# Last chunk of a Strassen MLP on Trainium2: a new order of the products, accumulating DMAs for the additions, the residual added in the output

## The chip, the cores and the metric

One core of one Trainium2 chip runs the kernel. The metric is the device time of one execution in microseconds (us), lower is better. TensorE (PE) multiplies, VectorE (DVE), ScalarE (ACT) and GpSimd (POOL) do the elementwise work, and DMAs are issued from the queues of SyncE (SP), ACT and POOL. Only a DMA issued on POOL adds to its destination here (`accum_op`).

## What is computed

One layer of an encoder over x of 512 x 2048 float32: convolution and attention, then the part that the change touches, the MLP:

```python
x = x + rms_norm(mix, post_mix_g[l])
h = rms_norm(x, pre_mlp_g[l])
f = jnp.square(jax.nn.relu(h @ w_up[l])) @ w_down[l]
x = x + rms_norm(f, post_mlp_g[l])
```

The last `rms_norm` needs the sum of squares over a whole row of 2048 columns of `f`; the row is then scaled by `r` (the reciprocal root) and by `post_mlp_g`, and the x of the line before (the residual, "x1" in the code) is added.

## The kernel before

**Chunks.** The MLP runs over 8 chunks of 1024 hidden columns. A chunk first makes its hidden block (`up`, two groups `g`), then multiplies it with its rows of `w_down` by a Strassen scheme of seven products, the table `PROD` (L30). The output f is cut into four quadrants (t, n): t = 0 holds rows 0 to 255 (row blocks of 128, j = 0 and 1), t = 1 the lower rows (j = 2 and 3), n the halves of 1024 columns. An entry of `PROD` names a ring buffer or the four Q tiles as weight source ("r" or "q"), the quarters of `w_down` that are summed, the form of the hidden block (a21, a11, t2, t5, t1, a22, t4), and the quadrants to which the product is added, with signs:

```python
PROD = (("q", (0, 0), "a21", {(1, 0): 1, (1, 1): -1}),
        ("r", ((0, 1), (1, 1)), "a11", {(0, 0): -1, (0, 1): 1}),
        ("q", (0, 1), "t2", {(1, 1): 1}),
        ("r", ((1, 1),), "t5", {(0, 1): -1, (1, 1): 1}),
        ("q", (1, 1), "t1", {(0, 0): 1, (1, 1): -1}),
        ("r", ((1, 0),), "a22", {(0, 0): -1, (1, 0): 1}),
        ("q", (1, 0), "t4", {(0, 0): 1}))
```

**One product** is four `down` steps of 12 matmuls; a step uses one weight piece of 128x1024 (half `nb` of the columns, half `h` of the depth). All numbers are float32 as a high and a low part: `ensure` (L196) makes them for a piece, a copy on ACT (L133) and a subtraction on DVE (L212). A ring holds three such pieces, so the split of piece s+2 stands ahead of step s. When a piece is split, `send_next` issues the next load into its buffer: a plain load on SP (L178), an accumulating one on POOL (L176). `split_form` (L746) splits the form, `sums` (L751) makes the next form in place.

**Adding products up.** After two steps half a product lies in two PSUM banks. `evac_down` (L784) takes it: in chunk 0 ACT copies it to one of seven accumulators, in chunks 1 to 6 DVE adds it, and in chunk 7 DVE adds or subtracts it to each quadrant `CA[q]` that `PROD` names (L794). Before chunk 7's products, `fold` combines the seven accumulators into the four quadrants; X[1] and X[2] are then free.

**The end.** Products run in the order 0 to 6 in chunk 7 also. Product 6 is left as four `fin` steps, one per row block j of the upper rows and half of the columns; its four pieces (blocks of Q) are split into Ah and Al. For a unit of 128x512, `stat` (L806) squares and sums on ACT, `gain` (L809) multiplies by `post_mlp_g` on POOL (on DVE for the last), and `finish_row` (L814) makes `r` by `tot_rstd` and writes x1 + r * m, three units of a row on DVE (L822) and one on ACT and POOL (L820), and stores them (L812). x1 of all four row blocks was stored to DRAM (`x1d`) ahead of the MLP and is read back by `load_x1` (L827) at the start of chunk 7's products.

**Order.** Each engine runs its instructions in the order in which the Python loop over `steps` emits them; `bg` adds work after a given step. A DMA in a queue waits for its semaphores with all that stands behind it.

Of the kernel before, what the change touches and what calls it, by code (L numbers as in the profile page):

```python
# [16 lines left out]
P = 128  # L17
# [48 lines left out]
def encoder_layer(ctx, tc, xT, xp, wst, pk, gmix, gmlp, rawb, maskc, out):  # L66
# [65 lines left out]
    def copy(o, i, scale=1.0):  # L132
        act(o, i, AF.Copy, scale=scale)  # L133
# [100 lines left out]
    for c in range(NCH):  # L234
        for g in range(2):
            fp = add_pieces(16, 2, 512, gain=True, mod=12)
            k0 = 0
            if c == 0 and g == 0:
                steps.append(dict(kind="up0", c=c, g=g, k=3, p=fp, n=16, cost=10.4))
                k0 = 4  # L240
            for k in range(k0, 16):
                steps.append(dict(kind="up", c=c, g=g, k=k, p=fp + k, n=16, cost=2.6))
        base = nw[0]
        nw[0] += 16
        quarter = lambda r, n, nb, h: base + 8 * r + 4 * n + 2 * nb + h
        for i, (buf, quarters, form, signs) in enumerate(PROD):
            last = c == NCH - 1 and i == NP - 1
            fp = len(pieces)
            for nb in range(2):
                for h in range(2):  # L250
                    if buf == "q":
                        b = add_block(("q", nb, h), [(quarter(*quarters, nb, h), i > 0)])
                    else:
                        b = add_block(None, [(quarter(*x, nb, h), n_ > 0) for n_, x in enumerate(quarters)])
                    res = None
                    if last:
                        e = 4 * nb + 2 * h
                        res = (Ah[:, e:e + 2, :].rearrange("p a b -> p (a b)"), Al[:, e:e + 2, :].rearrange("p a b -> p (a b)"))
                    add_piece(b, 0, 1024, None, res, 12)
            if last:  # L260
                for u in range(4):
                    steps.append(dict(kind="fin", c=c, i=i, tb=u // 2, nb=u % 2, p=fp, n=4, k=u, cost=2.6))
            else:
                for u in range(4):
                    steps.append(dict(kind="down", c=c, i=i, nb=u // 2, h=u % 2, p=fp + u, n=4, k=u, cost=2.6))
    n_ring = 0
    for blk in blocks:
        if not isinstance(blk["slot"], tuple):
# [490 lines left out]
    PREP = {(0, 1): lambda: sums("t5"), (0, 2): lambda: sums("d"), (0, 3): lambda: sums("t2"),  # L759
            (1, 1): lambda: split_form(2), (2, 1): lambda: split_form(3), (2, 2): lambda: sums("t1"),  # L760
            (3, 1): lambda: split_form(4), (3, 2): lambda: sums("t4"), (4, 1): lambda: split_form(5),
            (5, 1): lambda: split_form(6)}

    def up_set(c, g):
        return 4 * ((c + g) % 2)
# [15 lines left out]
    def hv(a, nb):  # L781
        return a[:, 1024 * nb:1024 * nb + 1024]

    def evac_down(c, i, nb):  # L784
# [18 lines left out]
    x1r = [f(Ah[:, 8 + 4 * j:12 + 4 * j, :]) for j in range(2)] + [f(Al[:, 8 + 4 * j:12 + 4 * j, :]) for j in range(2)]  # L803

    def stat(j, cb):
        act(X[2][:, 0:512], cunit(j, cb), AF.Square, accum_out=ss[:, 4 * j + cb:4 * j + cb + 1])  # L806

    def gain(j, cb, eng=None):
        (eng or nc.gpsimd).tensor_tensor(cunit(j, cb), cunit(j, cb), GM[:, 512 * cb:512 * cb + 512], ALU.mult)  # L809

    def store(j, cb, eng=None):
        (eng or nc.sync).dma_start(out[P * j:P * j + P, 512 * cb:512 * cb + 512], cunit(j, cb))  # L812

    def finish_row(j, last=False):  # L814
        r = tot_rstd(j, 20 if j % 2 else 32)
        for cb in (2, 0, 1, 3) if last else range(4):
            m = cunit(j, cb)
            if cb == 2:
                copy(m, m, r)
                nc.gpsimd.tensor_tensor(m, m, x1r[j][:, cb, :], ALU.add)  # L820
            else:
                V.scalar_tensor_tensor(m, m, r, x1r[j][:, cb, :], ALU.mult, ALU.add)  # L822
            if cb != 2:
                store(j, cb)
        store(j, 2, nc.scalar if last else nc.sync)

    def load_x1():  # L827
        for j in range(4):
            nc.scalar.dma_start(x1r[j], x1d[P * j:P * j + P].rearrange("p (a b) -> p a b", a=4))
        nc.gpsimd.dma_start(GM, bass.AP(tensor=gmlp.tensor, offset=gmlp.offset, ap=[[0, P], [1, D]]))  # L830

    su = first("up0")
    for j in range(4):
        bg.setdefault(su + 2 + j, []).append(lambda j=j: (x1_stat(j), nc.gpsimd.dma_start(x1d[P * j:P * j + P], X[j])))
    bg.setdefault(su + 7, []).append(lambda: rstd(sm[:, 0:4], 4, 1.0 / D, RMS_EPS, 16))
    bg_pe.setdefault(su + 9, []).append(r2_b)
    bg.setdefault(su + 10, []).append(lambda: [send_next(("q", nb, h), -1) for nb in range(2) for h in range(2)])
    for c in range(NCH):
        u1 = first("up", c=c, g=1)
        for i in range(2):  # L840
            bg.setdefault(u1 + 4 + 3 * i, []).append(lambda i=i: split_form(i))
        d0 = first("down", c=c, i=0)
        for (i, k), fn in PREP.items():
            bg.setdefault(d0 + 4 * i + k, []).append(fn)
# [6 lines left out]
    for i, rows, cbs in ((4, (0, 1), (2, 3)), (5, (2, 3), (2, 3)), (6, (2, 3), (0, 1))):  # L851
        for u in range(4):
            j, cb = rows[u % 2], cbs[u // 2]
            bg.setdefault(d7 + 4 * i + u, []).append(lambda j=j, cb=cb: (stat(j, cb), gain(j, cb)))
    for j in (2, 3):
        bg[d7 + 4 * 6 + 3].append(lambda j=j: finish_row(j))
# [4 lines left out]
    for si, s in enumerate(steps):  # L861
# [66 lines left out]
        elif kind == "oseq":  # L928
            j = s["j"]
            tk = slice(P * j, P * j + P)  # L930
            for kk in range(8):
                qq = pieces[p + kk]
                ah, al = Ah[:, 8 + kk, tk], Al[:, 8 + kk, tk]
                mm(acc[j], ah, qq["h"], start=False, stop=False, skip_group_check=True)
                mm(acc[j], al, qq["h"], start=False, stop=False, skip_group_check=True)
                mm(acc[j], ah, qq["l"], start=False, stop=(kk == 7), skip_group_check=True)
            if j >= 1:
                z_transpose(j - 1)
            oseq_post(j)
        elif kind in ("down", "fin"):  # L940
            pr = down_pair(s["c"], s["i"], s["nb"])
            fh, fl = mlp["FH"][s["i"] % 2], mlp["FL"][s["i"] % 2]
            todo = [(s["h"], q, tb) for tb in range(2)] if kind == "down" else [(h, pieces[p + 2 * s["nb"] + h], s["tb"]) for h in range(2)]
            for kk in range(2):
                for h, qq, tb in todo:
                    a = 2 * h + kk
                    fs = slice(P * tb, P * tb + P)
                    wh, wl = qq["h"][:, 512 * kk:512 * kk + 512], qq["l"][:, 512 * kk:512 * kk + 512]
                    st = kk == 0 and h == 0
                    en = kk == 1 and h == 1  # L950
                    mm(B[pr + tb], fh[:, a, fs], wh, start=st, stop=False, skip_group_check=True)  # L951
                    mm(B[pr + tb], fh[:, a, fs], wl, start=False, stop=False, skip_group_check=True)  # L952
                    mm(B[pr + tb], fl[:, a, fs], wh, start=False, stop=en, skip_group_check=True)  # L953
# [29 lines left out]
            elif kind == "up":  # L983
                evac_up(s["c"], s["g"])
        if kind == "down" and k % 2 == 1:
            evac_down(s["c"], s["i"], s["nb"])
        elif kind == "fin":
            j = s["tb"]
            m, b = cunit(j, s["nb"]), B[down_pair(s["c"], s["i"], s["nb"]) + j]
            V.tensor_tensor(m, m, b, ALU.add)  # L990
            stat(j, s["nb"])
            gain(j, s["nb"], V if k == 3 else None)
            if k % 2 == 1:
                finish_row(j, last=k == 3)
# [80 lines left out]
```

## Time and profile before

| What | us |
|---|---|
| Time, median of 3 runs (lowest, highest) | 2090.79 (2087.34, 2091.76) |
| The profiled execution: own time | 2092.75 |
| The profiled execution: span | 2091.0 |
| Start of chunk 7's products | 1981.1 |
| End of the last matmul | 2067.1 |

The profile is of one execution; its span begins with its first instruction, and times in a row count from there. Durations below come from it.

### The profile page before, as it was taken

The page shows a single profiled execution, that of the slowest core. Times are in us where ns is not written, and L with a number is a line of the kernel's source. Part 1 is how long each engine was busy: PE and PEld are TensorE (multiplying, and loading weights), DVE is VectorE, ACT ScalarE, POOL GpSimd, SP SyncE. Part 2 cuts the span into 40 slices and gives each one's busy share as a digit, 9 for nine tenths or more (in the row PEclk, how much of TensorE's full clock was granted, in tenths as well). Part 3 has the DMA queues.
Part 4 walks back from the last instruction along what each step waited for, and adds up shares of the span by engine and source line. Part 5 has one row for each costly group of instructions (what it writes and reads, how often), then busy time and mean ns, then how long its engine had stood idle before and what let it go on. Part 6 is the DMA issues. An engine that isn't in the chain of part 4 may idle for free.

```text
span 2091.0 us, 24692 instructions
## 1 busy us (share of the span) xinstructions
PE 2034.6 (97%) x9423; PEld 1684.8 (81%) x9423; DVE 1324.9 (63%) x1656; ACT 892.7 (43%) x1387; POOL 281.4 (13%) x275
## 2 busy tenths in 40 slices
PE   9999999997999999999999999999999999999994
PEld 7888887887788888888888888888888888888873
DVE  6899896976644644534843853763673573476498
ACT  6334444435653554633433433443343343343353
POOL 5110111112101301101101100100100110110124
PEclk9999999998999999999999999999999999999997
DMA  5223232222324256735844854763763773673592
GB/s 208 97 94 107 78 97 80 94 75 69 102 85 171 91 215 157 191 122 128 197 138 123 184 161 122 175 171 102 170 191 101 158 195 111 151 190 124 136 276 81
DMA packets 78584, 288.43 MB, mean 138 GB/s; under 512 B 8880, under 2 KB 9024, under 8 KB 76672
## 3 DMA queue, kind: packets, MB, share of 16 engines
q1 hardware_dynamic: 55440, 197.16, 27.9%
q0 software_dynamic: 21008, 81.16, 20.1%
q10 hardware_dynamic: 2016, 8.53, 1.1%
q8 instruction: 74, 1.21, 0.2%
q14 instruction: 46, 0.38, 0.1%
HBM read 278.42 MB, written 8.39 MB: 137 GB/s over the span
## 4 chain that ended last, share of the span: by engine, by line
PE 68%; DVE 3%; issue 2%; ACT 1%; POOL 0%; DVEq 0%; ACTq 0%; POOLq 0%
PE PS L898 33%; PE PS L951 9%; PE PS L953 9%; PE PS L952 9%; PE PS L927 2%; PE PS L926 2%; PE PS L925 2%; DVE WL L212 1%; DVE M L822 1%; DVE M L794 0%; PE PS L708 0%; PE PS L571 0%; DVE Al L212 0%; POOL M L679 0%; PE PS L557 0%
## 5 line engine op out<-in xcount | busy, mean ns | idle before, releaser
L898 PE MATMUL PS<-Ah,WH 128*128 128x512 f32 x1176 | 462.1, 393 | 3.7 <-ACT WH L133 3.7
L898 PE MATMUL PS<-Ah,WL 128*128 128x512 f32 x1176 | 459.8, 391 | 0.0
L898 PE MATMUL PS<-Al,WH 128*128 128x512 f32 x1176 | 459.6, 391 | 0.0
L133 ACT ACTIVATE WH<-WR 128x512 fp32r<-128x512 f32 (+2 forms) x312 | 207.4, 673 | 361.3 <-PE PS L898 155.3
L212 DVE TENSOR_TENSOR WL<-WR,WH 128x512 fp32r<-128x512 f32 (+2 forms) x312 | 255.4, 828 | 166.4 <-ACT WH L133 164.2
L215 DVE SCALAR_TENSOR_TENSOR WL<-WR,PRM,WH 128x512 fp32r<-128x512 f32 x170 | 128.2, 760 | 226.2 <-ACT WH L133 226.1
L898 PEld LDWEIGHTS PS<-Ah,WH 128*128 128x128 f32 x1176 | 222.5, 189 | 50.4 <-ACT WH L133 4.4
L898 PEld LDWEIGHTS PS<-Ah,WL 128*128 128x128 f32 x1176 | 222.3, 189 | 46.8
L898 PEld LDWEIGHTS PS<-Al,WH 128*128 128x128 f32 x1176 | 222.7, 189 | 45.4
L951 PE MATMUL PS<-WH,FH 128*128 128x512 f32 x588 | 232.7, 396 | 0.0
L953 PE MATMUL PS<-WH,FL 128*128 128x512 f32 x588 | 232.5, 395 | 0.0
L952 PE MATMUL PS<-WL,FH 128*128 128x512 f32 x588 | 232.1, 395 | 0.0
L133 ACT ACTIVATE WH<-WR,PRM 128x512 fp32r<-128x512 f32 x170 | 122.9, 724 | 246.7 <-PE PS L898 227.0
L212 DVE TENSOR_TENSOR WL<-Q,WH 128x1024 fp32r<-128x1024 f32 x83 | 101.3, 1222 | 97.2 <-ACT WH L133 97.2
L133 ACT ACTIVATE WH<-Q 128x1024 fp32r<-128x1024 f32 x83 | 88.2, 1063 | 136.1 <-PE PS L953 82.0
L215 DVE SCALAR_TENSOR_TENSOR WLX<-WR,PRM,WHX 128x512 fp32r<-128x512 f32 x86 | 64.1, 751 | 121.1 <-ACT WHX L133 121.1
L176 POOL DMA_DIRECT2D Q<-in_wst_dram x96 | 86.5, 901 | 376.0 <-DVE WL L212 238.9
L176 POOL DMA_DIRECT2D WR<-in_wst_dram x32 | 28.0, 875 | 808.5 <-DMA WR<-in_wst_dram 776.4
L898 PE MATMUL PS<-Al,WHX 128*128 128x512 f32 x344 | 135.9, 395 | 0.0
L898 PE MATMUL PS<-Ah,WHX 128*128 128x512 f32 x344 | 135.9, 395 | 0.0
L898 PE MATMUL PS<-Ah,WLX 128*128 128x512 f32 x344 | 135.6, 394 | 0.0
L953 PEld LDWEIGHTS PS<-WH,FL 128*128 128x128 f32 x588 | 110.2, 187 | 27.2
(200 smaller groups left out, 3506.7 us busy)
## 6 DMA issues: line engine op xcount, KB each, us to landing
WR<-in_wst_dram SPq DMA_DIRECT2D x335, 512.0 KB, 3.5
Q<-in_wst_dram POOLq DMA_DIRECT2D x96, 512.0 KB, 5.9
Q<-in_wst_dram SPq DMA_DIRECT2D x32, 512.0 KB, 3.6
WR<-in_wst_dram POOLq DMA_DIRECT2D x32, 512.0 KB, 5.7
X<-in_xp_dram POOLq DMA_DIRECT2D x4, 1024.0 KB, 8.9
x1d<-X POOLq DMA_DIRECT2D x4, 1024.0 KB, 9.3
out_dram<-M SPq DMA_DIRECT2D x15, 256.0 KB, 2.4
M<-in_xT_dram ACTq DMA_DIRECT2D x7, 512.0 KB, 4.7
```

Source lines behind the costliest of these rows:

```text
L133: act(o, i, AF.Copy, scale=scale)
L176: nc.gpsimd.dma_start(t, wst[i], accum_op=ALU.add)
L212: V.tensor_tensor(l, raw, f(h), ALU.subtract)
L215: V.scalar_tensor_tensor(l, raw, q["g"], f(h), ALU.mult, ALU.subtract)
L822: V.scalar_tensor_tensor(m, m, r, x1r[j][:, cb, :], ALU.mult, ALU.add)
L898: mm(acc[n], w, (Al if t == 1 else Ah)[:, k, :], start=(k == 0 and t == 0), stop=(lastk and t == 2), skip_group_check=True)
L925: mm(acc[j], ah[:, tk], q["h"], start=st, stop=False, skip_group_check=True)
L926: mm(acc[j], ah[:, tk], q["l"], start=False, stop=False, skip_group_check=True)
L927: mm(acc[j], al[:, tk], q["h"], start=False, stop=en, skip_group_check=True)
L951: mm(B[pr + tb], fh[:, a, fs], wh, start=st, stop=False, skip_group_check=True)
L952: mm(B[pr + tb], fh[:, a, fs], wl, start=False, stop=False, skip_group_check=True)
L953: mm(B[pr + tb], fl[:, a, fs], wh, start=False, stop=en, skip_group_check=True)
```

## The change

In chunk 7 the products run in the order 0, 2, 3, 4, 5, 1, 6 (`LAST`); "position i" below is the place in that order. At positions 0 to 3, ACT copies the two banks, scaled by the sign, into a half of X[1] or X[2], and a DMA on POOL adds that half to the quadrant; at positions 4 and 5 DVE adds as before. Row blocks 0, 2 and 3 of x1 are stored into `out` itself, and `add_row` adds r * m * gain to them by accumulating DMAs; only row block 1 goes through `x1d` and is finished in SBUF by `last_row`. The lower rows are finished at positions 4 and 5. The form a11 is split early into a free part of Ah and Al.

```diff
+LAST = (0, 2, 3, 4, 5, 1, 6)
-    x1d = drp.tile([T, D], F32, name="x1d")
+    x1d = drp.tile([P, D], F32, name="x1d")
...
+            pi = LAST[i] if c == NCH - 1 else i
+            buf, quarters, form, signs = PROD[pi]
...
+    def form_at(c, i):
+        if c == NCH - 1 and LAST[i] == 1:
+            return [t[:, 8:10, :].rearrange("p a (b c) -> p (a b) c", c=256) for t in (Ah, Al)]
+        return mlp["FH"][i % 2], mlp["FL"][i % 2]
...
+            plan = ((0, 0, 5), (0, 1, "t5"), (0, 2, "d"), (0, 2, "t2"), (0, 3, 1), (1, 1, 2), (1, 2, "t1"), (2, 1, 3), (2, 2, "t4"),
+                    (3, 1, 4), (5, 0, 6))
...
-            for q, sg in PROD[i][3].items():
+            for n_, (q, sg) in enumerate(PROD[pi][3].items()):
                 m = hv(CA[q], nb)
-                V.tensor_tensor(m, m, bank, ALU.add if sg > 0 else ALU.subtract)
+                if i < 4:
+                    st = hv(X[1 + n_], nb)
+                    copy(st, bank, float(sg))
+                    nc.gpsimd.dma_start(m, st, accum_op=ALU.add)
+                else:
+                    V.tensor_tensor(m, m, bank, ALU.add if sg > 0 else ALU.subtract)
...
+    def add_row(j, r, n):
+        V.scalar_tensor_tensor(wide(j, n), wide(j, n), r, gw(n), ALU.mult, ALU.mult)
+        nc.gpsimd.dma_start(out[P * j:P * j + P, 1024 * n:1024 * n + 1024].rearrange("p (a b) -> p a b", a=2), wide(j, n), accum_op=ALU.add)
+
+    def gain(cb):
+        V.tensor_tensor(cunit(1, cb), cunit(1, cb), GM[:, 512 * cb:512 * cb + 512], ALU.mult)
+
+    def last_row():
+        r = rows_rstd(1, 1, 20)
+        for cb in (2, 3, 0, 1):
+            m = cunit(1, cb)
+            V.scalar_tensor_tensor(m, m, r, x1r[:, cb, :], ALU.mult, ALU.add)
+            (nc.sync if cb % 2 else nc.scalar).dma_start(out[P:2 * P, 512 * cb:512 * cb + 512], m)
 
     def load_x1():
-        for j in range(4):
-            nc.scalar.dma_start(x1r[j], x1d[P * j:P * j + P].rearrange("p (a b) -> p a b", a=4))
-        nc.gpsimd.dma_start(GM, bass.AP(tensor=gmlp.tensor, offset=gmlp.offset, ap=[[0, P], [1, D]]))
+        nc.scalar.dma_start(x1r, x1d.rearrange("p (a b) -> p a b", a=4))
+        nc.sync.dma_start(GM, bass.AP(tensor=gmlp.tensor, offset=gmlp.offset, ap=[[0, P], [1, D]]))
...
+    for i, k, fn in [(4, 0, lambda: (stat(2, 2), stat(3, 2))), (4, 2, lambda: (stat(2, 3), stat(3, 3))),
+                     (4, 3, lambda: (stat(2, 0), stat(3, 0))),
+                     (5, 0, lambda: (stat(2, 1), stat(3, 1))), (5, 1, lambda: rows_rstd(2, 2, 32)),
+                     (5, 1, lambda: add_row(2, r23[:, 0:1], 1)), (5, 2, lambda: add_row(3, r23[:, 1:2], 1)),
+                     (5, 2, lambda: add_row(2, r23[:, 0:1], 0)), (5, 3, lambda: add_row(3, r23[:, 1:2], 0)),
+                     (5, 3, lambda: (stat(0, 2), stat(1, 2))), (6, 0, lambda: (stat(0, 3), stat(1, 3), gain(2), gain(3)))]:
```

**Place 1: POOL, the end of its queue.** Before, the last four loads of Q (here Q01 to Q11, for product 6) are followed by GpSimd's own multiplications and additions:

```order
L176 DMA Q01_5387<-in_wst_dram 128x1024 [waits DMASW5_49,DVE_49]
L176 DMA Q10_5388<-in_wst_dram 128x1024 [waits DMASW6_49,DVE_49]
L809 TENSOR_TENSOR M_67<-M_67,X0_68 128x512 [waits DMASW3_49,Activation_49]
L176 DMA Q11_5389<-in_wst_dram 128x1024 [waits DMASW7_49,DVE_49]
L809 TENSOR_TENSOR M_67<-M_67,X0_68 128x512 [waits Activation_49] x11
```

Now, from position 2's second half on (M is where the quadrants lie, X1 and X2 are X[1] and X[2], WR0 to WR3 the ring tiles):

```order
L816 DMA M_67<-X2_70 128x1024 [waits DMASW6_49,DMASW0_49,Activation_49]
L178 DMA Q10_5388<-in_wst_dram 128x1024 [waits DVE_49]
L178 DMA Q11_5389<-in_wst_dram 128x1024 [waits DVE_49]
L816 DMA M_67<-X1_69 128x1024 [waits DMASW1_49,Activation_49]
L816 DMA M_67<-X2_70 128x1024 [waits DMASW2_49,Activation_49]
L178 DMA WR0_73<-in_wst_dram 128x1024 [waits DMAHW1_49,DMASW3_49]
L178 DMA WR1_74<-in_wst_dram 128x1024 [waits DMAHW2_49,DMASW4_49]
L816 DMA M_67<-X1_69 128x1024 [waits DMASW5_49,Activation_49]
L816 DMA M_67<-X2_70 128x1024 [waits DMASW6_49,Activation_49]
L178 DMA WR2_75<-in_wst_dram 128x1024 [waits DMAHW3_49,DMASW7_49]
L178 DMA WR3_76<-in_wst_dram 128x1024 [waits DMAHW4_49,DMASW0_49]
L844 DMA out_0_dram<-M_67 128x2x512 [waits DMASW2_49,DMASW6_49,DMASW1_49,DVE_49]
```

GpSimd's arithmetic is gone; 14 additions of 128x1024 (L816) and 6 into `out` (L844) stand in the queue, and the four accumulating loads of product 1 (WR0 to WR3) come last among the loads.

**Place 2: DVE, from the form of product 6 to the last piece.** Before:

```order
L212 TENSOR_TENSOR Al<-Q_5386,Ah 128x1024
L749 TENSOR_TENSOR FL_5392<-G,FH_5390 128x1024
L794 TENSOR_TENSOR M<-M,PS 128x1024 x2
L212 TENSOR_TENSOR Al<-Q_5387,Ah 128x1024
L212 TENSOR_TENSOR Al<-Q_5388,Ah 128x1024
L794 TENSOR_TENSOR M<-M,PS 128x1024 x2
L212 TENSOR_TENSOR Al<-Q_5389,Ah 128x1024
```

Now, behind the split of WR3, the split of Q00 and the six small instructions that begin the reciprocal root of the lower rows:

```order
L318 TENSOR_TENSOR sm<-sm 128x2
L843 SCALAR_TENSOR_TENSOR M<-M,sm,X_68 128x2x512
L818 TENSOR_TENSOR M<-M,PS 128x1024 x2
L214 TENSOR_TENSOR Al<-Q_5387,Ah 128x1024
L843 SCALAR_TENSOR_TENSOR M<-M,sm,X_68 128x2x512 x2
L214 TENSOR_TENSOR Al<-Q_5388,Ah 128x1024
L843 SCALAR_TENSOR_TENSOR M<-M,sm,X_68 128x2x512
L818 TENSOR_TENSOR M<-M,PS 128x1024 x2
L214 TENSOR_TENSOR Al<-Q_5389,Ah 128x1024
```

The lower rows are scaled (L843) between the splits of the last product's pieces.

## Rows read from the trace of the kernel before

**Rows 1.** The page: span, and its part 1.
```profile
span 2091.0 us, 24692 instructions
...
PE 2034.6 (97%) x9423; PEld 1684.8 (81%) x9423; DVE 1324.9 (63%) x1656; ACT 892.7 (43%) x1387; POOL 281.4 (13%) x275
```
**Rows 2.** Busy time by stretch (stretch, its length, then each engine).
```profile
1981.10:2037.10 56.00, 55.98 (x241) 44.74 (x240) 52.43 (x46) 28.79 (x35) 13.79 (x15) 1.00 0.97 270
2037.10:2067.10 30.00, 24.46 (x95) 18.64 (x95) 26.97 (x27) 13.55 (x27) 14.32 (x10) 0.94 0.04 10
2067.10:2091.00 23.90, 0.01 (x1) 0.00 (x0) 16.65 (x34) 4.83 (x12) 10.01 (x7) 0.59 0.47 174
```
**Rows 3.** The chain of work that ended last: first matmul of chunk 7's products (start, length).
```profile
1981.09 0.23 PE PS L951
```
**Rows 4.** Timeline of ACT in chunk 0, first and last of thirteen evacuations (start, length).
```profile
824.93 1.03 ACT L133 ACTIVATE M<-PS 128x1024 f32<-128x1024 f32 x1 [1.63 <-PE PS L953]
...
889.05 1.06 ACT L133 ACTIVATE WH<-Q 128x1024 fp32r<-128x1024 f32 x1 [0.82 <-PE PS L953]
891.81 1.03 ACT L133 ACTIVATE M<-PS 128x1024 f32<-128x1024 f32 x1 [1.70 <-PE PS L953]
```
**Rows 5.** Timeline of PE in chunk 7: its waits, and the last matmul.
```profile
2039.11 0.50 PE L952 MATMUL PS<-WLX,FH 128*128 128x512 f32 x1 [2.02 <-DVE WLX L212]
...
2053.76 0.50 PE L952 MATMUL PS<-Al,FH 128*128 128x512 f32 x1 [2.51 <-DVE Al L212]
...
2059.38 0.50 PE L952 MATMUL PS<-Al,FH 128*128 128x512 f32 x1 [1.02 <-DVE Al L212]
...
2066.72 0.39 PE L953 MATMUL PS<-Ah,FL 128*128 128x512 f32 x1
```
**Rows 6.** Timeline of DVE in chunk 7.
```profile
1987.36 2.35 DVE L794 TENSOR_TENSOR M<-M,PS 128x1024 f32<-128x1024 f32 x2
1989.62 1.22 DVE L212 TENSOR_TENSOR WL<-WR,WH 128x1024 fp32r<-128x1024 f32 x1
...
2034.35 4.71 DVE L212 TENSOR_TENSOR WLX<-WR,WHX 128x1024 fp32r<-128x1024 f32 x1
...
2076.12 0.14 DVE L682 TENSOR_REDUCE sm<-sm 128x1 f32<-128x4 f32 x1
...
2077.69 3.08 DVE L822 SCALAR_TENSOR_TENSOR M<-M,sm,Al 128x512 f32<-128x512 f32 x3
2080.70 0.67 DVE L990 TENSOR_TENSOR M<-M,PS 128x512 f32<-128x512 f32 x1
2082.22 0.69 DVE L809 TENSOR_TENSOR M<-M,X 128x512 f32<-128x512 f32 x1 [0.85 <-ACT X L806]
...
2084.41 3.08 DVE L822 SCALAR_TENSOR_TENSOR M<-M,sm,Ah 128x512 f32<-128x512 f32 x3
```
**Rows 7.** Timeline of POOL in chunk 7: one of its multiplications.
```profile
2033.88 4.08 POOL L809 TENSOR_TENSOR M<-M,X 128x512 f32<-128x512 f32 x3
```
**Rows 8.** DMA queues from 1975 to 2042 (packets, MB, share of 16 engines), and issues.
```profile
q0 software_dynamic: 2016, 7.87, 58.6%
q10 hardware_dynamic: 576, 4.19, 16.3%
q1 hardware_dynamic: 1152, 4.19, 15.8%
...
Q<-in_wst_dram POOLq DMA_DIRECT2D x12, 512.0 KB, 8.2
```
**Rows 9.** DMA queues from 738 to 742: only the stores of x1 from SBUF run.
```profile
q0 software_dynamic: 222, 1.68, 104.0%
```
**Rows 10.** Timeline of POOL: the last loads of Q for product 2.
```profile
1984.96 0.87 POOL L176 DMA_DIRECT2D Q<-in_wst_dram  x1 [6.18 <-DVE WLX L212]
1986.60 0.87 POOL L176 DMA_DIRECT2D Q<-in_wst_dram  x1 [0.77 <-DVE WL L212]
```
**Rows 11.** Busy time by stretch; the last two numbers are DMA share and GB/s.
```profile
1987.00:1993.00 6.00, 6.00 (x27) 4.87 (x26) 6.00 (x6) 2.63 (x3) 1.03 (x2) 1.00 1.03 340
...
2011.00:2017.00 6.00, 6.00 (x28) 4.85 (x27) 5.93 (x6) 2.12 (x2) 0.00 (x0) 1.00 1.07 226
```
**Rows 12.** The page, part 6: issues (KB each, us from issue to landing).
```profile
WR<-in_wst_dram SPq DMA_DIRECT2D x335, 512.0 KB, 3.5
Q<-in_wst_dram POOLq DMA_DIRECT2D x96, 512.0 KB, 5.9
```

More of the change, by code (lines that the diff above doesn't have):

```diff
@@ L245, in encoder_layer @@
         quarter = lambda r, n, nb, h: base + 8 * r + 4 * n + 2 * nb + h
-        for i, (buf, quarters, form, signs) in enumerate(PROD):
+        for i in range(NP):
+            pi = LAST[i] if c == NCH - 1 else i
+            buf, quarters, form, signs = PROD[pi]
             last = c == NCH - 1 and i == NP - 1
@@ L261, in encoder_layer @@
                 for u in range(4):
[L262 removed]
+                    steps.append(dict(kind="fin", c=c, i=i, pi=pi, tb=u // 2, nb=u % 2, p=fp, n=4, k=u, cost=2.6))
             else:
                 for u in range(4):
[L265 removed]
+                    steps.append(dict(kind="down", c=c, i=i, pi=pi, nb=u // 2, h=u % 2, p=fp + u, n=4, k=u, cost=2.6))
     n_ring = 0
@@ L757, in sums, with prep @@
         V.tensor_tensor(o, a, b, op)
[L759 to L762, printed above, removed]
+    def prep(c):
+        if c < NCH - 1:
+            for i in range(2):
+                yield first("up", c=c, g=1) + 4 + 3 * i, lambda i=i: split_form(c, i)
+            plan = ((0, 1, "t5"), (0, 2, "d"), (0, 3, "t2"), (1, 1, 2), (2, 1, 3), (2, 2, "t1"), (3, 1, 4), (3, 2, "t4"),
+                    (4, 1, 5), (5, 1, 6))
+        else:
+            yield first("up", c=c, g=1) + 4, lambda: split_form(c, 0)
+            plan = ((0, 0, 5), (0, 1, "t5"), (0, 2, "d"), (0, 2, "t2"), (0, 3, 1), (1, 1, 2), (1, 2, "t1"), (2, 1, 3), (2, 2, "t4"),
+                    (3, 1, 4), (5, 0, 6))
+        d0 = first("down", c=c, i=0)
+        for i, k, what in plan:
+            yield d0 + 4 * i + k, (lambda what=what: sums(what)) if isinstance(what, str) else (lambda what=what: split_form(c, what))
     def up_set(c, g):
@@ L782, in hv, with evac_down @@
         return a[:, 1024 * nb:1024 * nb + 1024]
[L784 removed]
+    def evac_down(c, i, pi, nb):
         pr = down_pair(c, i, nb)
@@ L802, in encoder_layer @@
     GM = X[0]
-    x1r = [f(Ah[:, 8 + 4 * j:12 + 4 * j, :]) for j in range(2)] + [f(Al[:, 8 + 4 * j:12 + 4 * j, :]) for j in range(2)]
-    def stat(j, cb):
[L806 to L825, printed above, removed]
+    x1r = f(Ah[:, 12:16, :])
@@ new lines, in wide, with gw, rows_rstd @@
+    def wide(j, n):
+        return CA[j // 2, n].rearrange("p (n t c) -> p n t c", n=2, t=2)[:, :, j % 2, :]
+    def gw(n):
+        return GM[:, 1024 * n:1024 * n + 1024].rearrange("p (a b) -> p a b", a=2)
+    def stat(j, cb):
+        act(rb, cunit(j, cb), AF.Square, accum_out=ss[:, 4 * j + cb:4 * j + cb + 1])
+    def rows_rstd(j, n, col):
+        V.tensor_reduce(sm[:, 60:60 + n], ss[:, 4 * j:4 * (j + n)].rearrange("p (a b) -> p a b", b=4), AX.X, ALU.add)
+        return rstd(sm[:, 60:60 + n], n, 1.0 / D, RMS_EPS, col)
@@ L838, in encoder_layer @@
     for c in range(NCH):
[L839 to L844, printed above, removed]
+        for si, fn in prep(c):
+            bg.setdefault(si, []).append(fn)
     u0 = first("up", c=NCH - 1, g=0)
@@ L849, in encoder_layer @@
     bg.setdefault(d7 + 1, []).append(load_x1)
[L851 to L856, printed above, removed]
+    r23 = sm[:, 32:34]
+    for i, k, fn in [(4, 0, lambda: (stat(2, 2), stat(3, 2))), (4, 2, lambda: (stat(2, 3), stat(3, 3))),
[4 more added lines that the diff above has]
+                     (5, 3, lambda: (stat(0, 2), stat(1, 2))), (6, 0, lambda: (stat(0, 3), stat(1, 3), gain(2), gain(3)))]:
+        bg.setdefault(d7 + 4 * i + k, []).append(fn)
     gap_until = 0.0
@@ L991, in encoder_layer @@
             stat(j, s["nb"])
-            gain(j, s["nb"], V if k == 3 else None)
-            if k % 2 == 1:
-                finish_row(j, last=k == 3)
+            if j:
+                gain(s["nb"])
+            if k == 1:
+                r = rows_rstd(0, 1, 20)
+                for n in range(2):
+                    add_row(0, r, n)
+            elif k == 3:
+                last_row()
 def _layout(inputs):
```

18 lines of the change are left out of this document (10 added, 8 removed).

## The prediction

> **What bounds the kernel now.** The page comes first: PE is busy 97% of a span of 2091.0 us [rows 1], so a change in the last chunk can win only where PE waits there, or after its last matmul. The table by stretch shows where that is [rows 2]. Chunk 7's products begin at 1981.1 [rows 3]; I count from there and write T for it, so the span ends at T109.9. Up to 2037.1 PE is busy 55.98 of 56 us; in the next 30 us it lacks 5.5; after 2067.1 it has nothing to do for 23.9. What the seven products cost without a wait is seen in chunk 0, where ACT alone takes the banks: 12 half products lie between two evacuations 66.88 us apart [rows 4], so one is 5.573 and 14 are 78.0. Here the last matmul ends at 2067.1 [rows 5], T86.0: 8.0 us were lost. PE's timeline names for whom: 2.02, 2.51 and 1.02 us, each time for a DVE split [rows 5]; the rest is the slower clock behind a wait (0.94 on the mean) [rows 2]. DVE is busy 52.43 of 56 us and then 26.97 of 30 [rows 2]. Its instruction of 4.71 us, on a shape that takes 1.22 a few rows higher, runs beside GpSimd's multiplications [rows 6, 7]. So DVE is the bound, first by its queue and then by the finish of four row blocks.
>
> **What the change takes away.** At positions 0 to 3 (signs 2, 1, 2, 2, two halves each) 14 additions leave DVE; two cost 2.26 us from start to start [rows 6], 1.13 each, so 15.8 us. ACT takes 14 copies of 1.03 [rows 4]. For a product with two signs it then has four copies, four splits of 1.06 [rows 4] and a form, 9.4 of 11.15 us: it fits if nothing makes it wait. GpSimd's arithmetic goes, and DVE's collisions with it. Three row blocks no longer wait to be finished behind the last matmul.
>
> **The end, if no DMA is late.** The DVE order of place 2 sets it. Position 4 is multiplied at T55.7 (10 half products). DVE then has two additions, the split of WR2, the form of product 6 and the split of WR3: 5 x 1.13, so WR3 is split at T61.4, and PE wants it only at T64.1. Behind it stand four splits, four row scalings (L843; the form is new, priced as an addition of as many elements) and four additions, 12 x 1.13 = 13.6, and a reciprocal root, 1.57 from its first instruction to the scaling behind it [rows 6]: 15.2. Then 1.9 for the eight matmuls that need the last split, and for row block 0 an addition 0.6, its square 0.8, a root 1.5, two scalings 2.3; for row block 1 two rounds of addition, square and gain overlapped to 4.1; a root 1.5, four last operations at 0.67 each 2.7 (three took 3.08 with GpSimd in the way [rows 6]), and 3.5 from DVE's last instruction, 2087.5, to the span's end: 18.9. So **end = split of WR3 + 34.1**, here T95.5, 2076.6: 14.4 us less. PE ends inside the 18.9, at 7.5; it is no longer the bound of the tail. The change breaks even when WR3 is split at T75.8, 14 us late.
>
> **What the DMAs take.** From 1975 to 2042 the software queue moved 7.87 MB in 58.6% of 67 us, 39.3 us of all 16 engines; the plain queue 4.19 MB in 15.8%, 10.6 us [rows 8]. So a plain 512 KB takes 1.32. Of the 7.87 MB, 1.05 are the gains (plain, 2.65 us); the other 6.82 are 13 accumulating loads, 36.6 us: **2.82 each**, twice a plain one. All three queues together took 60.8 of these 67 us: little is free. Shares of 1.03 to 1.07 in saturated stretches [rows 11] say that some 3.5% overlaps.
>
> The price m of an addition from SBUF to SBUF stands in no row. Below it cannot well be under a plain copy: 1.32, or 1.30 by the stores of x1 from SBUF, 1.68 MB at 104% of 4 us [rows 9]. Above, it is the accumulating load of the same shape and queue, 2.82. It reads two things and writes one, as that load does, so it is nearest to it; since SBUF gave its bytes a little faster, I take **m = 2.7**. The Trainium skill says why such a DMA should cost double: the page "Collectives: The Full Stack", section "The bandwidth ceiling", has it that the add is free but needs two source reads on one ring. The accumulating loads here agree (2.82 against 1.32); by that rule m is 2.64 and the end 0.8 us earlier than mine, an estimate. No run here shows it for two sources in SBUF.
>
> **The sum.** The last loads of Q for product 2 are issued at T3.9 and T5.5 [rows 10] and, with x1 of one row block, hold the engines up to T13.8 (2 x 2.82 + 2.65). From there, all in front of or among the loads for product 1, come 8 Q and 4 WR accumulating loads, 33.8; 8 plain WR loads, 10.6; 14 additions, 37.8 (3 MB less of x1 are 7.9 us that the start no longer has). That is 82.2, with the overlap 79.4: WR3 lands at T93.2, where PE wanted it split at T64.1. POOL issues in order, and WR3 is the last load in place 1, so nothing can pass. On the way it shows as ACT waiting: the copy of position 1 into a half of X[1] must wait for the addition of position 0 from it, and behind that copy stands a split. With 2.3 for the split (1.06 and 1.22) WR3 is ready at T95.5, the end is T129.6, **2110.7: 19.7 us more** than 2091.0. The additions into `out` of the lower rows lie beside the last product; those of row block 0 are issued some 11 us before the end and land in 6 to 9 by the loads' 5.9 [rows 12]. The profiled execution's own time is 1.96 above the median of the runs; I move the median 2090.79 by the same 19.7: **2110**.
>
> With m = 1.32 the work is 62.9, with overlap 60.8: WR3 lands at T74.6, is ready at T76.9, end 2092.1, 1.1 more. With m = 2.82 and no overlap: 83.9, WR3 at T97.7, end 2115.2; some us for the slower clock behind long waits and for idle engines while POOL waits lead to 2120.
>
> **Rivals.** First, **faster: the DMAs keep up.** If packets of several accumulating DMAs overlap so that each costs the engines no more than a copy, loads and additions together are 34 x 1.32 = 44.9 and WR3 lands at T58.7, before PE wants it. Then the end is 2076.6, 14.4 us less: 2076. It decides at a landing of T73.5, that is at 60 us for the whole work. For it speaks that ACT kept pace with the copies in chunk 0, and that DVE is plainly the bound now; against it, that the accumulating loads did not overlap so: in the full stretch they landed 8.2 us after issue [rows 8], over the run 5.9 [rows 12]. By the fit in the page "DMA: Bandwidth & Descriptors" of the Trainium skill, section "Anatomy of one DMA", 2 us and then 436 GB/s, 512 KB would move in 1.2 us, which would put this case ahead of mine, an estimate; the trace does not agree for accumulating loads, which land after 5.9 us where plain ones need 3.5 [rows 12]. Second, **no change: only the additions are cheap** (m near 1.32): the gain at the tail is eaten by the late WR3, 2092. Speaks for it that no HBM is read; against it that the destination is read as before. That the change does not do what it says can be left out: both places show the instructions.
>
> **Chances.** Late DMAs as summed: 0.70, own range 2099 to 2120. No change: 0.12, 2088 to 2099. Faster: 0.18, 2072 to 2088. The range that holds 8 in 10 leaves out most of the faster case: 2084 to 2120. A measurement can tell 0.2%, 4.2 us. Faster by more than that takes the faster case and a little of the second: 0.19; within it 0.10; slower the rest, 0.71.
>
> **What would show it.** In the new profile the DMA share should be near 1 from 1990 to 2075, not to 2040; PE should have waits of 5 to 10 us from position 1 on, behind splits on ACT and DVE that themselves wait for DMAs; WR3's split should stand near T95, the last matmul near T118, 15 to 20 us before the end. The forecast is wrong if PE runs through positions 1 to 3 without waits, if an addition takes well under 2 us of the 16 engines, or if the split of WR3 lies before T76.

## The result, and the profile after

The change takes 2114.97 us (median of 4 runs, 2113.48 to 2116.50) against 2090.24 us of the kernel before, run beside it (4 runs, 2087.34 to 2091.76): a ratio of 1.0121, 95% interval 1.0108 to 1.0134. It is slower by 24.7 us where 19.7 was forecast, and inside the range. The profiled execution took 2115.64 us with a span of 2113.8. Its last chunk begins 1.3 us earlier than before's, by the evacuation ahead of the products, here in the change and then before:

```profile
1978.48 2.70 ACT L793 ACTIVATE G<-PS 128x512 f32<-128x512 f32 x4 [3.40 <-DVE PS L792]
```

```profile
1979.76 2.70 ACT L774 ACTIVATE G<-PS 128x512 f32<-128x512 f32 x4 [3.40 <-DVE PS L773]
```

From there to the end it is 135.3 us against 111.2: 24.1 more. Where the last chunk begins differs by some us from one execution to the next, so kernels are compared below by this length, called L, of one execution each (two executions of one kernel, further down, have 99.9 and 100.0).

The page of the change, span and part 1, against [rows 1]:

```profile
span 2113.8 us, 24667 instructions
...
PE 2043.5 (97%) x9423; PEld 1689.3 (80%) x9423; DVE 1299.7 (61%) x1636; ACT 902.5 (43%) x1396; POOL 270.3 (13%) x275
```

DVE's work fell by 25 us, POOL's by 11, and the kernel is slower. Busy time by stretch (PE, PEld, DVE, ACT, POOL, granted clock, DMA share, GB/s), against [rows 2]:

```profile
1981.10:2037.10 56.00, 46.87 (x184) 36.47 (x183) 29.86 (x26) 32.07 (x34) 19.14 (x22) 0.91 0.99 215
2037.10:2067.10 30.00, 18.07 (x65) 13.06 (x63) 6.66 (x6) 6.82 (x10) 4.40 (x5) 0.83 1.06 241
2067.10:2091.00 23.90, 15.65 (x52) 11.73 (x52) 21.05 (x25) 13.21 (x26) 5.71 (x5) 0.85 0.50 78
2091.00:2113.80 22.80, 10.13 (x32) 7.74 (x32) 13.34 (x29) 4.63 (x14) 2.39 (x2) 0.65 0.70 136
```

In the first 86 us no compute engine is full any more: PE 65 of 86 us, DVE 37, where before it had 79. What is full is the last column but one, the DMA engines: 1.06 over 30 us in which they had 0.04 before. The same table in steps of 6 us shows where that begins and ends:

```profile
1987.00:1993.00 6.00, 3.96 (x18) 2.86 (x16) 4.60 (x4) 3.26 (x5) 2.46 (x3) 1.00 1.00 182
...
2059.00:2065.00 6.00, 5.70 (x17) 4.56 (x18) 3.64 (x4) 0.18 (x1) 0.00 (x0) 0.65 1.06 231
2065.00:2071.00 6.00, 2.72 (x10) 1.72 (x9) 1.81 (x2) 4.21 (x10) 0.86 (x1) 0.92 0.76 161
2071.00:2077.00 6.00, 6.00 (x23) 4.81 (x22) 5.71 (x6) 4.76 (x8) 0.00 (x0) 0.80 0.29 58
```

PE's timeline, four of its waits (start, length, in brackets the idle time before it and what ended that), against [rows 5]:

```profile
1993.13 0.50 PE L977 MATMUL PS<-WH,FH 128*128 128x512 f32 x1 [2.17 <-ACT FH L135]
...
2023.99 0.79 PE L977 MATMUL PS<-WH,FH 128*128 128x512 f32 x1 [5.96 <-ACT WH L135]
...
2058.04 0.79 PE L977 MATMUL PS<-WH,FH 128*128 128x512 f32 x1 [10.29 <-ACT WH L135]
...
2083.86 0.80 PE L978 MATMUL PS<-Al,FH 128*128 128x512 f32 x1 [2.77 <-DVE Al L214]
```

The first is for the form of position 1, which waits for sums on DVE and not for a DMA. The two long ones, at positions 3 and 4, wait for splits on ACT. ACT's own timeline says what held those:

```profile
2021.06 1.94 ACT L135 ACTIVATE X<-PS 128x1024 f32<-128x1024 f32 x2 [9.34 <-DMA M<-X]
...
2055.57 0.63 ACT L836 ACTIVATE rb<-M 128x512 f32<-128x512 f32 x1 [11.95 <-DMA M<-X]
...
2066.73 0.63 ACT L836 ACTIVATE rb<-M 128x512 f32<-128x512 f32 x1 [7.55 <-DMA M<-X]
```

`M<-X` is an accumulating addition of the change. At 2021 a copy waits for its staging half; at 2055 and 2066 a square of the statistics waits for a sum that the DMAs have not finished, and the split of the next block stands behind it in ACT's order. Last, product 1's last block on its way, from its accumulating load on POOL to the split on DVE:

```profile
2068.10 0.86 POOL L178 DMA_DIRECT2D WR<-in_wst_dram  x1 [12.64 <-DMA WR<-in_wst_dram]
```

```profile
2075.23 1.23 DVE L214 TENSOR_TENSOR WLX<-WR,WHX 128x1024 fp32r<-128x1024 f32 x1 [0.28 <-ACT WHX L135]
```

The load lands 5.3 us after its issue, at 2073.4. The block is split by 2076.46, T95.4, and the span ends 37.3 us later. The page's part 6 (KB each, median us from issue to landing), against [rows 12]:

```profile
M<-X POOLq DMA_DIRECT2D x14, 512.0 KB, 12.5
```

### The profile page after: what moved, and what is told of

Its sections match the earlier page's. It is cut to its first block, busy times and chain, and to the rows that moved or that the text cites. A ratio compares the mean times of both kernels' runs of the same rounds, so it can differ in the third digit from the quotient of the medians.

```text
span 2113.8 us, 24667 instructions
## 1 busy us (share of the span) xinstructions
PE 2043.5 (97%) x9423; PEld 1689.3 (80%) x9423; DVE 1299.7 (61%) x1636; ACT 902.5 (43%) x1396; POOL 270.3 (13%) x275
## 4 chain that ended last, share of the span: by engine, by line
PE 66%; DVE 3%; DMA 3%; issue 2%; ACT 1%; POOL 0%; DVEq 0%; ACTq 0%; POOLq 0%
PE PS L924 33%; PE PS L977 9%; PE PS L979 9%; PE PS L978 9%; PE PS L953 2%; PE PS L952 2%; PE PS L951 2%; DMA M<-X 1%; DMA WR<-in_wst_dram 1%; DVE WL L214 0%; DVE M L843 0%; DVE M L818 0%; ACT X L135 0%; PE PS L712 0%; PE PS L575 0%
## 5 line engine op out<-in xcount | busy, mean ns | idle before, releaser
L977 PEld LDWEIGHTS PS<-WH,FH 128*128 128x128 f32 x580 | 110.2, 190 | 46.1 <-ACT WH L135 17.5
L978 PEld LDWEIGHTS PS<-WL,FH 128*128 128x128 f32 x580 | 110.0, 190 | 29.4 <-DVE WL L214 3.0
```

## The experiments

All are edits of the change and run the whole kernel. "Split to end" is from the end of the last split of product 1 (at position 5) to the span's end. Each ratio is to the kernel before as it ran beside that kernel; a kernel with one run has none.

| kernel | median us (runs) | ratio to before, 95% | L us | split to end us |
|---|---|---|---|---|
| before | 2090.79 (3) | | 111.2 | |
| the change | 2114.97 (4) | 1.0121, 1.0108 to 1.0134 | 135.3 | 37.3 |
| additions on VectorE | 2093.45 (10) | 1.0014, 1.0005 to 1.0023 | 112.4 | 37.3 |
| no additions | 2092.41 (1) | | 111.8 | 37.6 |
| plain copies | 2098.26 (1) | | 117.9 | 36.2 |
| statistics late | 2116.87 (4) | 1.0127, 1.0110 to 1.0144 | 138.2 | 37.3 |
| order 0, 3, 2, 5, 4, 1, 6 | 2082.05 (5) | 0.9967, 0.9954 to 0.9980 | 102.5 | 37.4 |
| the same, splits of product 6 first | 2080.92 (7) | 0.9957, 0.9945 to 0.9970 | 101.5 | 37.9 |
| DMA additions at two positions | 2097.98 (4) | 1.0043, 1.0028 to 1.0058 | 119.5 | 37.0 |
| old order | 2078.31 (5) | 0.9942, 0.9929 to 0.9956 | 100.0 | |
| old order, 14 DMA additions | 2102.02 (2) | 1.0055, 1.0037 to 1.0073 | 120.4 | |
| old order, 4 DMA additions | 2079.49 (5) | 0.9949, 0.9937 to 0.9962 | 100.1 | |

### The additions: all of them, none, and as copies

```diff
-                if i < 4:
+                if i < 0:
```

> All products are computed; the additions of positions 0 to 3, which the change makes by DMAs on POOL's queue, are made on VectorE again (14 instructions of 1.13 us, 15.8 us of VectorE). The order of the products and the additions into the output stay as in the change. Theory (the DMA engines' work of the accumulating additions, 14 times some 2.7 us, makes the loads of the last blocks late): the DMA share stays under 1 after T70, product 1's block is split near T64 instead of T95, and the span ends near 2080 us (2077 to 2087), some 10 us before the kernel before and 33 before the change. Rival (the new order itself, or the additions into the output behind it, is the loss): the span stays at 2100 or more.

The span ended at 2092.1, L is 112.4. The additions by DMA cost 135.3 - 112.4 = 22.9 us; but neither expectation held, for what is left of the change wins nothing either. The rows of this run, on POOL, ACT and DVE, say why:

```profile
2034.22 0.86 POOL L178 DMA_DIRECT2D WR<-in_wst_dram  x1 [8.32 <-DMA WR<-in_wst_dram]
...
2045.41 0.86 POOL L178 DMA_DIRECT2D WR<-in_wst_dram  x1 [5.27 <-DMA WR<-in_wst_dram]
```

```profile
2043.91 1.06 ACT L135 ACTIVATE WHX<-WR 128x1024 fp32r<-128x1024 f32 x1 [9.43 <-DMA WR<-in_wst_dram]
```

```profile
2053.55 1.23 DVE L214 TENSOR_TENSOR WLX<-WR,WHX 128x1024 fp32r<-128x1024 f32 x1 [0.29 <-ACT WHX L135]
```

Product 1's blocks are late without any addition: the first is wanted when PE's matmuls of position 4 end, at 2041.7, and lands at 2043.9. Its plain load (SP) and then its accumulating load (POOL) may start only when position 4's splits have emptied the four WR buffers, since the new order puts product 5 and product 1, the two that use them, next to each other. The chain of work that ended last puts, in this run, 22.9% of its time from 2030 to the end on these loads. New theory: the additions cost 23 us and this reuse of buffers some 10, and what else the change does wins part of that back.

```diff
-                    nc.gpsimd.dma_start(m, st, accum_op=ALU.add)
```

> Leaves out the 14 accumulating DMAs of positions 0 to 3 (these products are not added up); the ScalarE copies out of PSUM that feed them stay. Theory (the DMA work binds): as with the additions on VectorE, span 2075 to 2083 us, with less VectorE work than there. Rival (the order, or ScalarE's extra copies, cost the time): over 2091.

The theory's 2075 to 2083 is missed: the span ended at 2090.6, and the time is what the rival gave for the order or the copies. L is 111.8, 0.6 less than with the additions on VectorE. So 14 copies more on ACT and 15.8 us less work on VectorE together win next to nothing while product 1's loads are late.

```diff
-                    nc.gpsimd.dma_start(m, st, accum_op=ALU.add)
+                    nc.gpsimd.dma_start(m, st)
```

> The 14 DMAs of positions 0 to 3 copy instead of adding (the products overwrite one another); queue, bytes written, waits and order are those of the change. Theory (engine work counts: a plain 512 KB copy at 1.32 us of 16 engines instead of 2.7): 19 us less DMA work, product 1's block is split near T77, and the span ends at 2090 to 2097 us. Rival (it is the chain of waits on each DMA's landing, in order on POOL's queue, whatever the DMA does): within 4 us of the change's 2113.8.

The span ended at 2096.5, at the upper end of what the theory gave: most of the loss goes when the same DMAs copy, with the same waits in the same order. So it is what the addition costs the engines, and not the chain of landings. The queues of this run from 2011 to 2017 (packets, MB, share of 16 engines):

```profile
q1 hardware_dynamic: 414, 1.50, 61.0%
q0 software_dynamic: 259, 0.95, 39.1%
```

All 16 engines are full and move 409 GB/s; 0.95 MB in 39.1% of 6 us is 1.30 us for 512 KB from SBUF to SBUF, the prediction's lower bound. (q0 is the queue of POOL's DMAs, q1 that of SP's.) In the change q0 nearly alone fills the engines, here from 2000 to 2010 and from 2030 to 2040:

```profile
q0 software_dynamic: 551, 2.00, 101.9%
```

```profile
q0 software_dynamic: 559, 2.05, 107.1%
```

That is 2.67 and 2.74 us for 512 KB, additions and accumulating loads together. For additions alone the landings speak: of the first two, issued one behind the other at 1986.8 and 1987.7, the second landed 2.5 us after the first, of the next two 2.7 us after; with copies in place of the first two it was 1.3. The Trainium skill's page "Collectives: The Full Stack", section "The bandwidth ceiling", has it that the add of a reduction needs two source reads. The trace agrees: 2.67 and 2.74 where twice a plain transfer is 2.64, now with both sources in SBUF also.

### How the loss grows with the number of additions

```diff
-                if i < 4:
+                if i < 2:
```

> The change with accumulating DMAs for the additions of positions 0 and 1 alone (6 of the 14); positions 2 and 3 add on VectorE. Theory (each addition is 2.7 us of work for engines that are full): 8 x 2.7 x 0.97 = 21 us less DMA work than in the change, less what then goes idle, so that most of the loss is gone: span 2092 to 2100. Rival (ScalarE's in-order waits behind a late addition, which stand at positions 1 to 4 alike): the loss falls in proportion, 6/14 of 21.7 us, or 2101, and more if the first position's waits weigh most.

2097.98 us, as the theory had it. By L the first six additions cost 7.1 us (1.2 each), the other eight 15.8 (2.0 each). The first six find idle time: with all additions on VectorE the DMA share from 1993 to 2023 is 0.97, 0.83, 0.81, 0.54 and 0.53 in steps of 6 us, so 7.9 us are free for the 16.2 that six additions take, an estimate.

### The statistics that wait on ScalarE

```diff
-    for i, k, fn in [(4, 0, lambda: (stat(2, 2), stat(3, 2))), (4, 2, lambda: (stat(2, 3), stat(3, 3))),
-                     (4, 3, lambda: (stat(2, 0), stat(3, 0))),
+    for i, k, fn in [(5, 0, lambda: (stat(2, 2), stat(3, 2))), (5, 0, lambda: (stat(2, 3), stat(3, 3))),
+                     (5, 0, lambda: (stat(2, 0), stat(3, 0))),
```

> The three pairs of statistics copies that follow position 4 on ScalarE (they read sums that the DMAs finish) go behind position 5; all else is the change. Theory (DMA work in total sets when the last block lands): ScalarE no longer holds the split of product 5's last block for 12 us, but the engines are as full; span 2107 to 2113. Rival (the in-order wait of ScalarE for the additions is what makes product 1's last load late): the load goes out some 10 us earlier and the span falls by 8 to 15 us, to 2099 to 2106.

2116.87 us and L 138.2: both expectations missed, the theory's by 2 us on the slow side. The last accumulating load for product 1 went out at 2056.26 instead of 2068.10, 9.9 us earlier by each chunk's beginning, so the squares had delayed it:

```profile
2056.26 0.86 POOL L178 DMA_DIRECT2D WR<-in_wst_dram  x1 [2.94 <-DMA WR<-in_wst_dram]
```

But it landed 13.4 us after its issue, at 2069.7, where the change's landed after 5.3: only 1.7 us earlier by each chunk's beginning. So far the theory holds: the sum of the DMA work sets the landing, whenever the load goes out. The missed part is behind it, for the eight squares now stand one behind another ahead of the last split on ACT, from 2069.20 to 2075.1:

```profile
2069.20 0.61 ACT L836 ACTIVATE rb<-M 128x512 f32<-128x512 f32 x1
...
2075.09 1.04 ACT L135 ACTIVATE WHX<-WR 128x1024 fp32r<-128x1024 f32 x1
```

The block had landed 5.4 us before its split began. One delay took the other's place. What a place behind the last split would give was not tried and stays open.

### The order of the products

```diff
-LAST = (0, 2, 3, 4, 5, 1, 6)
+LAST = (0, 3, 2, 5, 4, 1, 6)
...
-            plan = ((0, 0, 5), (0, 1, "t5"), (0, 2, "d"), (0, 2, "t2"), (0, 3, 1), (1, 1, 2), (1, 2, "t1"), (2, 1, 3), (2, 2, "t4"),
-                    (3, 1, 4), (5, 0, 6))
+            plan = ((0, 0, 5), (0, 1, "t5"), (0, 2, 1), (0, 3, "d"), (1, 0, "t2"), (1, 1, 2), (2, 1, 3), (2, 2, "t1"),
+                    (3, 1, 4), (3, 2, "t4"), (5, 0, 6))
```

(Additions on VectorE, and the statistics of each column block moved to where it is complete.)

> As the run with the additions on VectorE, but with the last chunk's products in the order 0, 3, 2, 5, 4, 1, 6: the two products that take the four WR buffers, 5 and 1, no longer stand next to each other, so that the loads for product 1 can start some 11 us earlier; the same five products stand at positions 0 to 4. Theory (in that run the loads of product 1 waited for the buffers that product 5's splits free, and the end is the last split of product 1 plus 37.4): PE's wait for the first block of product 1 goes, the last block is split at T64 to T67 instead of T73.6, and the span ends at 2082 to 2087. Rival (VectorE's queue sets the end, whatever the loads do): within 2 us of 2092.1.

The wait for product 1's first block is gone, its first accumulating load goes out 14.1 us earlier (12.1 by each chunk's beginning), and the last split runs at 2041.66:

```profile
2020.17 0.86 POOL L178 DMA_DIRECT2D WR<-in_wst_dram  x1 [10.16 <-DMA WR<-in_wst_dram]
```

```profile
2041.66 1.23 DVE L214 TENSOR_TENSOR WLX<-WR,WHX 128x1024 fp32r<-128x1024 f32 x1 [0.29 <-ACT WHX L135]
```

The span ends at 2080.3, 1.7 us under the expected 2082 to 2087, as this chunk began 1.9 us earlier; L falls by 9.9 to 102.5. But the new order takes away a second wait too. PE's waits with the additions on VectorE, then in this run:

```profile
PE PS L977 <- ACT WHX L135: 3.3, 1, 3.3
PE PS L977 <- ACT FH L135: 2.8, 1, 2.8
```

```profile
PE PS L978 <- DVE Al L214: 6.4, 3, 3.6
PE PS L978 <- DVE WLX L214: 1.0, 1, 1.0
```

FH is the form of position 1. In the change's order that is product 2's, which stands behind sums on VectorE, two of them just ahead of it; PE waits 2.8 us for it and then runs at the lower clock (0.72 granted on the mean from 1993 to 1999). So the five products of positions 0 to 4 took 60.9 us (1980.86 to 2041.73) and here 57.8 (1978.95 to 2036.72). Some 3.1 of the 9.9 us are this wait, and some 6.8 the loads; no run takes away one without the other.

```diff
-            if kind == "down" and s["c"] == NCH - 1 and s["i"] == NP - 2 and k:
-                ensure(p + 3)
+            if kind == "down" and s["c"] == NCH - 1 and s["i"] == NP - 2:
+                ensure(p + 4 + (k > 0))
```

> As the run before it, with product 6's four splits issued one to two steps earlier, three of them ahead of the row scalings on VectorE. Theory (in the tail TensorE waits for these splits behind scalings and additions, 5.9 us in three waits, and then runs at the slower clock): these waits shrink to under 2 us and the span ends 3 to 6 us earlier, 2077 to 2083. Rival (the sum of VectorE's work behind the last block decides, whatever its order): within 1.5 us of the run before it.

Here the split of product 1's last block takes the buffer of its first, so the first block's matmuls wait for that split and use the last block's weights; the amount of work is the same. PE's waits of this run:

```profile
PE PS L978 <- DVE WLX L214: 2.8, 2, 1.8
PE PS L977 <- ACT WHX L135: 2.1, 1, 2.1
```

The waits for product 6's splits, 6.4 us in three before, are gone, 3.9 us of new ones stand at product 1's first block, and the time is 1.1 us less, inside the scatter of the runs: the rival held. VectorE is busy 27.4 of the 33.5 us from the last split to its own last instruction in the run before and 28.6 of 34.0 here: that work, in whatever order it stands, sets the end.

```diff
-LAST = (0, 2, 3, 4, 5, 1, 6)
+LAST = (0, 1, 2, 3, 4, 5, 6)
...
-        if c < NCH - 1:
+        if c < NCH:
...
+                     (6, 0, lambda: (stat(2, 1), stat(3, 1))), (6, 0, lambda: rows_rstd(2, 2, 32)),
+                     (6, 0, lambda: (add_row(2, r23[:, 0:1], 1), add_row(3, r23[:, 1:2], 1))),
+                     (6, 1, lambda: (add_row(2, r23[:, 0:1], 0), add_row(3, r23[:, 1:2], 0)))]:
```

> The products in the old order 0 to 6 with the old forms, all additions on VectorE; of the change there remain the residual in the output and the additions into it, with the statistics moved to where each row block is complete (rows 2 and 3 after position 5). Theory (the new order put product 1's loads next to product 5's and so late; the residual in the output shortens the tail by itself): no wait for WR loads, last matmul near 2066, span 2078 to 2088. Rival (without the new order four row blocks are still finished behind the last matmul, and the new additions only replace work that lay beside it): 2090 or more.

> The kernel of the run in the old order (residual in the output, additions on VectorE) once more, timed: if that look holds, 2072 to 2077 us, 0.6 to 0.9% faster than the kernel before; if it was a chance of one execution, within 0.2% of it.

The first run gave 2074.54 us with a span of 2072.8 and the last matmul at 2053.5: the rival (2090 or more) fell, and the theory (2078 to 2088, last matmul near 2066) was too slow by 5 us and more. The five timed runs gave 2078.31, a little above the expected 2072 to 2077 and 0.58% faster than before: the fastest kernel of this study. Its L was 99.9 and 100.0; the first run's last chunk only began 2.3 us earlier. Busy time by stretch of the timed run, against [rows 2]:

```profile
1981.10:2037.10 56.00, 56.00 (x243) 45.17 (x242) 54.47 (x50) 30.07 (x38) 7.86 (x10) 1.00 0.78 186
2037.10:2067.10 30.00, 17.71 (x75) 13.63 (x74) 25.56 (x44) 11.47 (x27) 7.28 (x6) 0.88 0.51 84
```

PE runs through: its first product matmul starts at 1976.33, its last ends at 2055.80. That is 79.5 us where the products need 78.0 without a wait [rows 4]; before it was 86.2, from 1980.93, where PE's timeline has the first of them (the chain of [rows 3] takes it up 0.16 later). Behind it stand 19.4 us instead of 23.9. So 6.7 of the 11.2 us lie in the products and 4.5 behind them. Without GpSimd's multiplications no split takes 4.71 us [rows 6] or more than 1.23; those of WR take 1.22 here:

```profile
L214 DVE TENSOR_TENSOR WLX<-WR,WHX 128x1024 fp32r<-128x1024 f32 x4 | 4.9, 1215 | 0.0
```

How much of the 11.2 us is GpSimd's arithmetic gone and how much the residual in the output was not tried apart.

### The additions in the old order

```diff
-                if i < 0:
+                if i < 4:
```

> As that kernel, with the additions of positions 0 to 3 by accumulating DMAs as in the change (14 of them), in the old order. Theory (the engines' work counts in any order): 37.8 us more for the engines, of which some 9.5 find them idle before 2029 and the rest pushes the last loads of product 6, which land near 2031 without them, to 2055 to 2062, past the 2035 to 2045 where they are split; span 2084 to 2096. Rival (the additions hurt only because the new order makes product 1 reuse its buffers late): 2078 or less.

L is 120.4, 20.4 more than without them; the new order gave 22.9. So the rival fell: the additions cost their engine work in any order. The theory's time was 2 us short and its place wrong. The DMA share is 1.04 to 1.08 from 1993 to 2059 but for one step of 0.78, so the engines are full here too. PE's longest wait, 8.3 us, is not at product 6's loads but at position 3, behind copies out of PSUM that wait for their staging halves:

```profile
PE PS L977 <- ACT WH L135: 8.3, 1, 8.3
```

```profile
2037.09 1.94 ACT L135 ACTIVATE X<-PS 128x1024 f32<-128x1024 f32 x2 [10.34 <-DMA M<-X]
```

With the additions of position 0 alone:

```diff
-                if i < 0:
+                if i < 1:
```

> As the kernel in the old order, with the additions of position 0 alone by accumulating DMAs (4 of them, 10.8 us of engine work beside some 9.5 us in which the engines were idle before 2029; VectorE loses 4.5 us of work). Theory (VectorE's queue is the bound there, and the engines have room for four): 1 to 4 us faster than without them, span 2069 to 2072. Rival (any added transfer makes a load late that something waits for): 2 us slower or more, 2075 to 2081.

2079.49 us, L 100.1: no difference that can be measured from 2078.31. Four additions are hidden, and 4.5 us less work on VectorE wins nothing either. Both expectations missed: VectorE is no longer the bound there. PE's products again take 79.5 us (1979.91 to 2059.37), with one wait of 1.0.

## Why the prediction was right, and where it was not

**The price of an addition: right.** 2.7 was taken between 1.32 and 2.82; 2.67 and 2.74 were measured (loads among them), 2.5 to 2.7 between landings of additions, and 1.30 for a copy. Had it been a copy's price, the forecast was a WR3 ready at T76.9 and an end at 2092.1; the run with plain copies had T79.2 and 2096.5.

**The full engines: right.** A share near 1 was expected from 1990 to 2075; it was 0.99 to 1.08 from 1987 to 2065 and ran out by 2073. The last block was forecast to land at T93.2 and be ready at T95.5; it landed at 2073.4, T92.3, ACT came to it behind two squares at 2074.15, and it was ready at T95.4. By the chunk's own beginning, 1.3 us earlier, that is 1.2 later than forecast. That it fits so closely is in part luck: the last block did not go through full engines to the end (the share is 0.76 from 2065 to 2071 and 0.29 from 2071 to 2077) but came late through the squares, to within 1.7 us of where full engines alone put it in the run with the statistics late.

**The end behind the split: the term that was mis-sized.** "end = split of WR3 + 34.1" measured 36.2 to 37.9 in eight kernels. In the run with the loads apart, DVE's chain took 15.5 (forecast 15.2). The matmuls that need the last split took 3.9 instead of 1.9: they follow a wait of 3.63 us and run at the lower level of the clock, 1.2 GHz (granted 0.50 from 2058.5 to 2062.2), 0.43 us from start to start where 0.23 is usual. PE's timeline there:

```profile
2058.42 0.79 PE L978 MATMUL PS<-Al,FH 128*128 128x512 f32 x1 [3.63 <-DVE Al L214]
2059.01 0.63 PE L979 MATMUL PS<-Ah,FL 128*128 128x512 f32 x1
2059.44 0.63 PE L977 MATMUL PS<-Ah,FH 128*128 128x512 f32 x1
2059.87 0.63 PE L978 MATMUL PS<-Al,FH 128*128 128x512 f32 x1
```

What stands behind took 18.1 instead of 17.0, 0.4 of it after DVE's last instruction. In the change the same tail is 37.3, 3.2 over the forecast, and its span ends 3.1 after the forecast 2110.7. By L the miss is 4.4 (24.1 where 19.7 was forecast): 3.2 in this tail and 1.2 in the split ahead of it.

**The end if no DMA is late: wrong for this order, the step that failed.** T61.4 for the split of WR3 and 2076.6 for the end took the loads as ready. With the loads of products 5 and 1 apart that split ended at 2042.89, T61.8, and the span at 2080.3, the 3.3 us of the tail later; by that chunk's own beginning, 2.0 us before that of the kernel before, the split was 2.4 late. In the change's own order, additions on VectorE, it ended at T73.7 and the span at 2092.1. Two terms were put at nothing. Position 4 was to be multiplied by T55.7, ten half products without a wait; it ended at 2041.73, T60.6, behind the wait for the form at position 1. And the sum counted the loads for product 1 as work and not as steps that must wait for a buffer. The forecast of the end survived by luck, for with 14 additions the engines were full past those waits; what it gave to each cause did not. The additions were priced at 34.1 (2110.7 less 2076.6) and cost 22.9. By L, in steps that were each run: the residual in the output, additions on VectorE, old order, -11.2; the order with loads apart +2.5; loads next to each other, with the form at position 1, +9.9; additions by DMA +22.9; together +24.1.

**The rivals.** "The DMAs keep up" was put at 2076. Even with no additions at all the change's order gives 2092.41, so that rival's time was wrong by the same step. "Only the additions are cheap", 2092, is 4 us under the run with plain copies.

**Signs.** PE's waits of 5.96 and 10.29 us behind ACT came as expected, but at positions 3 and 4 and not from position 1 on, and the longer one stands behind squares of the statistics, a queue that the prediction did not name. The last matmul ends at 2102.1, T121.0, 11.7 us before the end; the sum itself implied 11.4, while the list of signs said 15 to 20, which was wrong.

## What to carry to other kernels

Before an addition is given to a DMA, price it as two transfers of its bytes (2.7 us against 1.3 for 512 KB here) and add it to what the engines already carry in that stretch, not over the kernel: four fitted beside the loads here and cost nothing, fourteen cost 20 to 23 us. When an order of work is changed, list for each load the instruction that frees its buffer, and for each form the sums ahead of it; here the step that needs two loads for each buffer had become the neighbour of one that uses the same buffers, and a form that needs several sums had come to position 1. And change one thing at a time: the part of this change that paid, the residual already in the output and row blocks scaled and added there without GpSimd's arithmetic, was hidden under the two that didn't.

## What the runs showed that was not expected

The time from the last split to the end hardly moved (36.2 to 37.9 us) while the split itself moved by 36 us between kernels; so the one time that had to be forecast was that of the split.

Less work on VectorE, which was full before, won nothing twice, 15.8 us with late loads and 4.5 us in the old order, and splits issued earlier won 1.1 us. Each time another bound stood close behind: the loads, PE itself, whose products took 79.5 us where 78.0 is the least, or the same work in another place.

Engines that are full at a share near 1 moved 409 GB/s with copies and loads mixed (plain copies, 2011 to 2017) and 178 to 281 GB/s with mostly accumulating ones: the share says that they are busy, the GB/s what they are busy with.
